# One layer of a hybrid decoder trunk: gates and projections branch by branch, the output projection last, one pool of 4 KB buffers

## The chip, the cores and the metric

The kernel runs on one core of a Trainium2 chip. The metric is the device time in microseconds (us). Three timed executions of the kernel before took 506.86, 507.49 and 507.55 us, so the median is 507.49 us.

## What is computed

The reference is one layer on 512 positions (rows) of 1024 channels, followed by a final RMSNorm:

```
h = RMSNorm(x);  u = h @ w_in          # split into the inputs, gate paths (z) and gate logits below
ya = pool_mixer(a_x)   * silu(a_z)     # trailing-window means of 2/4/8/16, then a 128x128 mix per group
yb = window_attention  * silu(b_z)     # window 128, 8 query heads, 2 key/value heads, sinks
yc = block_attention   * silu(c_z)     # blocks of 256; at 512 positions this is causal attention, 8 heads
ga, gb, gc = split(sigmoid(gate_logits))            # 3 x 1024 columns
merged = ga * (ya @ w_proj_a) + gb * (yb @ w_proj_b) + gc * (yc @ w_proj_c)
out = RMSNorm(x + merged @ w_out)
```

Every matrix product is done in three float32r products, with each operand split into a rounded high part and the rest: high x high, high x low, low x high (`mm3`).

## The kernel before

Activations lie transposed, channels on the 128 partitions and 512 positions in the free dimension. A weight block is 128x1024 float32 (512 KB). It comes in over SP's DMA queue into one of four raw buffers (`wr`). ScalarE (ACT) casts it into its high part `wh` and VectorE (DVE) subtracts to get the low part `wl` (three buffers each). `weights(name)` keeps this two blocks ahead of the use, and each split block starts the load four blocks further on. The host lays the blocks out in the order in which they are used.

The program has four stages.

1. An opening, whose order is written out by hand (`manual_schedule`, until the seventh input block): loads of x, the first input blocks, RMSNorm.
2. 34 input blocks (`UNITS`). A block is 8 chunks of three matmuls, and the work of both attentions and of the pooling mixer is spread over the chunks by a table (`todo`, `tick`). Keys and queries are copied into place by DMAs on SP's queue (`moves`, L263-266) before the first score can use them.
3. Gates and projections (L525-603), channel block by channel block: for j = 0..7 the three gates (24 matmuls of 512 columns each, sigmoid), then the three projections of 12 matmuls each, and their weighted sum, which is split into `merged[j]`. For j = 1 to 5 the first gate is followed by `project_out(j - 1)`: eight products of three matmuls, each into a PSUM bank of its own turn and added by DVE to `acc`, which holds x.
4. A tail (L606-684): for the last three blocks the output projection is summed in PSUM, and row block by row block DVE adds it to `acc`, ACT squares, GpSimd (POOL) multiplies by the final gain, DVE and ACT scale, and SP stores.

After the opening a planner orders each engine's instructions at build time. It takes the program's order as the priority, and it issues an instruction early when its inputs and its buffer are there. Buffers come from pools with a number of slots per tag. A tile takes any free slot and gives it back after its last reader. Before, 2 KB tiles have the tag `t2` (31 slots), 4 KB pairs the tag `two` (9 slots), the normalised activations `hT` have 16 fixed places, and x, the values `vt` and `acc` follow one another in one place of 20 KB (tag `v`). PSUM has four tags of two banks: `big`, `PV`, `S`, `T`.

Of the kernel before, what the change touches and what calls it, by code (L numbers as in the profile page):

```python
# [14 lines left out]
P = 128  # L15
D = 1024
# [29 lines left out]


def weight_blocks():

    blocks = [(u, 1024) for u in UNITS]  # L50
    late = []
    for j in range(KT):
        blocks.append((("ga", j), 1024))
        if late:
            blocks.append((("wo", late.pop()), 1024))
        blocks += [(("gb", j), 1024), (("gc", j), 1024), (("pab", j), 1024), (("pc", j), 512)]
        if j < KT - TAIL:
            late.append(j)
    blocks += [(("wo", j), 1024) for j in range(KT - TAIL, KT)]
    return blocks  # L60
# [3 lines left out]
def trunk(ctx: ExitStack, tc: tile.TileContext, a, out: bass.AP):  # L64
# [17 lines left out]
    blocks = weight_blocks()  # L82
    index = {name: n for n, (name, _) in enumerate(blocks)}
# [6 lines left out]

    def load_upto(n):
        while done["load"] <= min(n, len(blocks) - 1):
            m = done["load"]
            cols = blocks[m][1]
            nc.sync.dma_start(raw_tile(m)[:, :cols], a["w"][m][:, :cols])
            done["load"] += 1
# [9 lines left out]
    def split_upto(n):  # L106
        while done["split"] <= min(n, len(blocks) - 1):
            m = done["split"]
            parts_of(m)
            split_cols(m, slice(0, blocks[m][1]))  # L110
            done["split"] += 1
            load_upto(m + 4)
# [6 lines left out]
    def split(src, name, two=None):  # L119
        hi, lo = (t2(F32R, name + "h"), t2(F32R, name + "l")) if two is None else (two[:, 0, :], two[:, 1, :])  # L120
        nc.scalar.copy(hi, src)
        nc.vector.tensor_sub(lo, src, hi.bitcast(F32))
        return hi, lo

    def mm3(ps, lh, ll, rh, rl, start, stop):
        nc.tensor.matmul(ps, lh, rh, start=start, stop=False)  # L126
        nc.tensor.matmul(ps, lh, rl, start=False, stop=False)  # L127
        nc.tensor.matmul(ps, ll, rh, start=False, stop=stop)  # L128
# [17 lines left out]
    xT = [t2(F32, f"xT{k}") for k in range(KT)]  # L146
# [10 lines left out]
    xn = pool.tile([P, NT, D], F32, name="xn", tag="v", bufs=1, padded_shape=[P, 5, 1024])  # L157
    for t in range(NT):
        nc.sync.dma_start(xn[:, t, :], a["x"][t * P:(t + 1) * P, :])
# [27 lines left out]
    for k in range(KT):  # L187
        hi, lo = t2(F32R, f"xgh{k}"), t2(F32R, f"xgl{k}")
# [22 lines left out]
    def square(t):  # L211
        junk = pool.tile([P, 1280], F32, name=f"junk{t}", tag="p", bufs=2)
        nc.scalar.activation(junk[:, :D], xn[:, t, :], AF.Square, accum_out=small[:, t:t + 1])
# [17 lines left out]
    def normed(k):  # L231
        tmp = t2(F32, f"ht{k}")
        nc.vector.scalar_tensor_tensor(tmp, xT[k], g_sb[:, k:k + 1], rstd_bc, op0=OP.mult, op1=OP.mult)
        hi, lo = const(f"hh{k}", [P, S], F32R), const(f"hl{k}", [P, S], F32R)
        nc.scalar.copy(hi, tmp)
        hT.append((hi, lo, tmp))
# [9 lines left out]
    vt = []  # L246

    def evacuate(u, ps):
# [5 lines left out]
        if kind in ("cq", "ck", "bq", "bk"):  # L254
            hi, lo = split(ps, f"{kind}{i}")
            top, low = slice(0, HD), slice(HD, P)
            if kind[1] == "q":
                two = parts[u] = pair(F32R, f"{kind}{i}two")
                moves = ((two, top, 0, hi, top), (two, low, 0, lo, top),
                         (two, low, 1, hi, low), (two, top, 1, lo, low))  # L260
            else:
                his, los = parts[u] = pair(F32R, f"{kind}{i}his"), pair(F32R, f"{kind}{i}los")
# [4 lines left out]
        elif kind == "cz":  # L267
            full[u] = t2(F32, f"{kind}{i}")
# [5 lines left out]
        else:  # L274
            full[u] = t2(F32, f"{kind}{i}")
# [4 lines left out]
    def value_tile():  # L280
        if not vt:
            vt.append(pool.tile([P, NT, 10, 2, HD], F32R, name="vt", tag="v", bufs=1))
        return vt[0]

    def keep_v(t, ps):

        p3 = ps.rearrange("p (h d) -> p h d", h=8)
        hi, lo = value_tile()[:, t, :8, 0, :], value_tile()[:, t, :8, 1, :]
# [3 lines left out]
    def turn_v(u):  # L292
# [5 lines left out]
        p4 = ps.rearrange("p (t h d) -> p t h d", t=NT, h=2)  # L298
        for n in range(2):
            hi, lo = value_tile()[:, :, 8 + n, 0, :], value_tile()[:, :, 8 + n, 1, :]  # L300
# [19 lines left out]
    def pool_mix(i):  # L320
# [7 lines left out]
        full["oa", i] = t2(F32, f"oa{i}")  # L328
        nc.scalar.activation(full["oa", i], ps, AF.Copy, scale=psc_sb[:, i:i + 1])
# [10 lines left out]
    def head(s):  # L340
        if s not in heads:
# [6 lines left out]
            h.v = n if h.moba else 8 + h.par  # L348
# [43 lines left out]
    def turn(s, b):  # L392
# [19 lines left out]
        hi, lo = t2(F32R, f"pth{s}_{b}"), t2(F32R, f"ptl{s}_{b}")  # L412
# [11 lines left out]
    def weigh(s, half):  # L424
# [9 lines left out]
        for n in (0, 1) if half == 0 else (2, 3):  # L434
            b, j, x, w, q0 = steps[n]
            v = vt[0][:, j, h.v, :, :]
# [3 lines left out]
        if half == 1:  # L440
            kind = "oc" if h.moba else "ob"
            if h.par == 0:
                full[kind, h.block] = t2(F32, f"{kind}{h.block}")
            rest = t2(F32, f"rest{s}")
            nc.scalar.copy(rest[:HD, :], h.o[HD:, :])
            nc.vector.tensor_add(full[kind, h.block][h.rows, :], h.o[:HD, :], rest[:HD, :])

# [23 lines left out]
    for s in range(16):  # L471
# [6 lines left out]
        for half, d in enumerate(WEIGH):  # L478
            at(c + d, weigh, s, half)
    chunk = 15  # L480
# [34 lines left out]
    acc = pool.tile([P, NT, D], F32, name="acc", tag="v", bufs=1, padded_shape=[P, 5, 1024])  # L515
    for t in range(NT):
        nc.gpsimd.dma_start(acc[:, t, :], a["x"][t * P:(t + 1) * P, :])

    fg_two = pair(F32, "fg")
    fg_sb = [fg_two[:, n, :] for n in range(2)]  # L520
# [4 lines left out]
    y = {}  # L525

    def gated(n, i):
        o, z = full["o" + n, i], full[n + "z", i]
        nc.vector.tensor_mul(o, o, z)
        y[n, i] = split(o, f"y{n}{i}")  # L530

    sig_two = {}

    def gate(n, j, sig, m):
        wh, wl = weights(("g" + n, j))
        ps = bank("big", f"ps_g{n}{j}")
        for k in range(KT):
            c = slice(k * P, (k + 1) * P)
            mm3(ps, wh[:, c], wl[:, c], *hT[k], k == 0, k == KT - 1)
        if m == 0:  # L540
            sig_two[j] = pair(F32, f"sig{j}")
        sig.append(sig_two[j][:, m, :] if m < 2 else t2(F32, f"sig{n}{j}"))
        last_sig = nc.scalar.activation(sig[m], ps, AF.Sigmoid)
        if (n, j) == ("c", KT - 1):
            with tc.issue_after(last_sig.ins):
                nc.scalar.sqrt(one, one)

    merged = {}

    def project(j, sig):  # L550
        m = t2(F32, f"m{j}")
        for b, n in enumerate("abc"):
            if b < 2:
                wh, wl = weights(("pab", j))
                at0 = b * 512
            else:
                wh, wl = weights(("pc", j))
                at0 = 0
            ps = bank("T", f"ps_p{n}{j}")
            for i in range(4):  # L560
                c = slice(at0 + i * P, at0 + (i + 1) * P)
                mm3(ps, wh[:, c], wl[:, c], *y[n, i], i == 0, i == 3)
            sg = sig[b]
            if b == 0:
                nc.vector.tensor_mul(m, ps, sg)
            else:
                t = t2(F32, f"t{n}{j}")
                nc.vector.tensor_mul(t, ps, sg)
                nc.vector.tensor_add(m, m, t)
        merged[j] = split(m, f"mg{j}", pair(F32R, f"mg{j}"))  # L570

    turns = [0]

    def out_bank(name):
        turns[0] += 1
        return bank(("S", "PV")[turns[0] % 2], name)

    def project_out(j):
        wh, wl = weights(("wo", j))
        for t in range(NT):  # L580
            for hf in range(2):
                ps = out_bank(f"ps_y{j}_{t}{hf}")
                tc_, c = slice(t * P, (t + 1) * P), slice(hf * 512, (hf + 1) * 512)
# [3 lines left out]
    for j in range(KT):  # L587
        sig = []
        gate("a", j, sig, 0)
        if j == 0:  # L590
            for i in range(4):
                gated("a", i)
        if 0 < j <= KT - TAIL:
            project_out(j - 1)
        gate("b", j, sig, 1)
        if j == 0:
            for i in range(4):
                gated("b", i)
        gate("c", j, sig, 2)
        if j == 0:  # L600
            for i in range(4):
                gated("c", i)
        project(j, sig)


    last = range(KT - TAIL, KT)  # L606
    wo = [weights(("wo", j)) for j in last]
    accs = {}

    ss = const("ss", [P, 48])  # L610
    prod = {}

    def tail_mm(t, hf, js, lo=0, hi=512):
        tc_, c = slice(t * P, (t + 1) * P), slice(hf * 512 + lo, hf * 512 + hi)
        if (t, hf, lo) not in accs:
            accs[t, hf, lo] = bank({0: "S", 1: "PV", 2: "T", 3: "big"}[t] if lo == 0 else "S", f"ps_z{t}{hf}{lo}")
        for j in js:
            mm3(accs[t, hf, lo][:, :hi - lo], merged[j][0][:, tc_], merged[j][1][:, tc_],
                wo[j - last[0]][0][:, c], wo[j - last[0]][1][:, c], j == last[0], j == last[-1])
# [4 lines left out]
    def tail_sum(t, hf, part, lo=0, hi=512):  # L624

        c = slice(hf * 512 + lo, hf * 512 + hi)
        add = nc.vector.tensor_add(acc[:, t, c], acc[:, t, c], accs[t, hf, lo][:, :hi - lo])  # L627
        junk = pool.tile([P, 1280], F32, name=f"sq{t}{part}", tag="p", bufs=2)
        nc.scalar.activation(junk[:, lo:hi], acc[:, t, c], AF.Square, accum_out=col(t, part))
# [4 lines left out]
    def tail_mul(t, hf, eng, lo=0, hi=512):  # L634
        if lo == 0:
# [119 lines left out]
```

## Time and profile before

| what | value |
|---|---|
| median of three executions | 507.49 us |
| the profiled execution | 506.78 us, its span 505.0 us |
| TensorE (PE) busy | 494.8 us, 98% of the span |
| DVE busy | 305.1 us, 60% |
| ACT busy | 232.4 us, 46% |
| POOL busy | 33.3 us, 7% |
| granted TensorE clock | full speed (2.4 GHz) in every slice until the end; mean 0.994 |
| moved by DMA | 59.94 MB, mean 119 GB/s |

The profile counts matmuls as busy until their modelled end, so a busy PE need not be at its peak. What an idle or a waiting engine costs is read from who waits for it.

### The profile page before, as it was taken

The page shows a single profiled execution, that of the slowest core. Times are in us where ns is not written, and L with a number is a line of the kernel's source. Part 1 is how long each engine was busy: PE and PEld are TensorE (multiplying, and loading weights), DVE is VectorE, ACT ScalarE, POOL GpSimd, SP SyncE. Part 2 cuts the span into 40 slices and gives each one's busy share as a digit, 9 for nine tenths or more (in the row PEclk, how much of TensorE's full clock was granted, in tenths as well). Part 3 has the DMA queues.
Part 4 walks back from the last instruction along what each step waited for, and adds up shares of the span by engine and source line. Part 5 has one row for each costly group of instructions (what it writes and reads, how often), then busy time and mean ns, then how long its engine had stood idle before and what let it go on. Part 6 is the DMA issues. An engine that isn't in the chain of part 4 may idle for free.

```text
span 505.0 us, 6455 instructions
## 1 busy us (share of the span) xinstructions
PE 494.8 (98%) x2297; PEld 402.7 (80%) x2297; DVE 305.1 (60%) x605; ACT 232.4 (46%) x452; POOL 33.3 (7%) x72
## 2 busy tenths in 40 slices
PE   8999999999999999999999999999999999999993
PEld 5788888888888888888888887888888888888882
DVE  5558877676788975558556626455272563433376
ACT  6655665656565675559464223132222222323344
POOL 2052000000021100000100000000000000000022
PEclk9999999999999999999999999999999999999997
DMA  8999427743622122210552231313232321313004
GB/s 258 398 257 242 147 74 179 197 125 92 174 72 104 43 83 85 83 56 29 199 182 80 85 123 64 125 65 123 85 104 85 102 85 64 125 64 125 0 2 167
DMA packets 22368, 59.94 MB, mean 119 GB/s; under 512 B 3200, under 2 KB 4224, under 8 KB 22336
## 3 DMA queue, kind: packets, MB, share of 16 engines
q1 hardware_dynamic: 21312, 56.63, 35.6%
q0 software_dynamic: 880, 2.89, 1.6%
q8 instruction: 18, 0.29, 0.2%
q14 instruction: 14, 0.11, 0.1%
q10 hardware_dynamic: 144, 0.00, 0.0%
HBM read 47.98 MB, written 2.10 MB: 99 GB/s over the span
## 4 chain that ended last, share of the span: by engine, by line
PE 95%; DVE 2%; ACT 1%; DMA 1%; issue 0%; SPq 0%; ACTq 0%
PE ps_o L438 3%; PE ps_gc L126 3%; PE ps_gb L126 3%; PE ps_gc L127 3%; PE ps_ga L128 3%; PE ps_gb L127 3%; PE ps_gc L128 3%; PE ps_gb L128 3%; PE ps_ga L127 3%; PE ps_ga L126 3%; PE ps_t L410 3%; PE ps_y L126 2%; PE ps_y L128 2%; PE ps_y L127 2%; PE ps_s L369 2%; PE ps_s L368 2%
## 5 line engine op out<-in xcount | busy, mean ns | idle before, releaser
L103 ACT CAST wh<-wr 128x1024 fp32r<-128x1024 f32 (+2 forms) x88 | 83.5, 952 | 166.5 <-PE ps_gc L127 35.7
L104 DVE TENSOR_TENSOR wl<-wr,wh 128x1024 fp32r<-128x1024 f32 (+2 forms) x84 | 91.6, 1095 | 94.1 <-ACT wh L103 93.7
L377 ACT ACTIVATE p<-p,st 128x128 f32<-128x128 f32 (+2 forms) x64 | 33.4, 523 | 34.5 <-DVE st L375 34.4
L585 DVE TENSOR_TENSOR acc<-acc,ps_y 128x512 f32<-128x512 f32 x40 | 24.8, 684 | 15.7 <-PE ps_y L128 15.7
L421 DVE TENSOR_TENSOR ptl<-ps_t,pth 128x512 fp32r<-128x512 f32 (+3 forms) x56 | 26.5, 476 | 7.3 <-ACT pth L420 6.8
L420 ACT CAST pth<-ps_t 128x512 fp32r<-128x512 f32 (+3 forms) x56 | 23.4, 418 | 12.8 <-PE ps_t L410 7.7
L128 PE MATMUL ps_ga<-hh,wl 128*128 128x512 f32 x64 | 25.3, 395 | 0.0
L127 PE MATMUL ps_ga<-hl,wh 128*128 128x512 f32 x64 | 25.3, 395 | 0.0
L128 PE MATMUL ps_gb<-hh,wl 128*128 128x512 f32 x64 | 25.3, 395 | 0.0
L126 PE MATMUL ps_gc<-hh,wh 128*128 128x512 f32 x64 | 25.3, 395 | 0.0
L127 PE MATMUL ps_gc<-hl,wh 128*128 128x512 f32 x64 | 25.3, 395 | 0.0
L128 PE MATMUL ps_gc<-hh,wl 128*128 128x512 f32 x64 | 25.3, 395 | 0.0
L126 PE MATMUL ps_gb<-hh,wh 128*128 128x512 f32 x64 | 25.3, 395 | 0.0
L127 PE MATMUL ps_gb<-hl,wh 128*128 128x512 f32 x64 | 25.3, 395 | 0.0
L126 PE MATMUL ps_ga<-hh,wh 128*128 128x512 f32 x64 | 25.3, 395 | 0.0
L637 POOL TENSOR_TENSOR yo<-acc,fg 128x512 f32<-128x512 f32 x5 | 6.4, 1294 | 241.7 <-DVE acc L627 239.4
L410 PE MATMUL ps_t<-ident,p 128*128 128x128 f32 x136 | 21.3, 272 | 0.0
L390 DVE TENSOR_SCALAR p<-p,st 128x128 f32<-128x128 f32 (+2 forms) x64 | 19.9, 358 | 0.5
L410 PEld LDWEIGHTS ps_t<-ident,p 128*128 128x128 f32 x136 | 16.7, 141 | 3.7
L438 PE MATMUL ps_o<-pth,vt 128*128 128x256 f32 (+1 forms) x64 | 17.8, 296 | 0.0
L438 PE MATMUL ps_o<-ptl,vt 128*128 128x256 f32 (+1 forms) x64 | 17.7, 300 | 0.0
L375 DVE CUSTOM_DVE_ANT_0 p<-ps_s,mask_c,nscale 128x128 f32<-128x128 f32 (+3 forms) x32 | 16.5, 545 | 1.7 <-PE ps_s L369 1.6
(390 smaller groups left out, 1263.4 us busy)
## 6 DMA issues: line engine op xcount, KB each, us to landing
wr<-in_w SPq DMA_DIRECT2D x72, 512.0 KB, 3.3
xT<-in_xT SPq DMA_DIRECT2D x8, 256.0 KB, 4.7
xn<-in_x SPq DMA_DIRECT2D x4, 512.0 KB, 8.7
wr<-in_w SPq DMA_DIRECT2D x8, 256.0 KB, 2.6
acc<-in_x POOLq DMA_DIRECT2D x4, 512.0 KB, 6.5
out<-yo SPq DMA_DIRECT2D x8, 256.0 KB, 2.3
wr<-in_w SPq DMA_DIRECT2D x8, 128.0 KB, 4.4
ck0his<-ck0h SPq DMA_DIRECT2D x4, 128.0 KB, 6.0
```

The costliest lines, as they stand in the source:

```text
L103: nc.scalar.copy(w_hi[n][:, c], raw_w[n][:, c])
L104: (nc.gpsimd if 4 <= n < 8 else nc.vector).tensor_sub(w_lo[n][:, c], raw_w[n][:, c], w_hi[n][:, c].bitcast(F32))
L126: nc.tensor.matmul(ps, lh, rh, start=start, stop=False)
L127: nc.tensor.matmul(ps, lh, rl, start=False, stop=False)
L128: nc.tensor.matmul(ps, ll, rh, start=False, stop=stop)
L377: exps.append(nc.scalar.activation(dst, dst, AF.Exp, bias=h.st[:, i:i + 1], scale=-1.0, accum_out=h.st[:, 4 + i:5 + i]))
L390: nc.vector.tensor_scalar_mul(dst, dst, h.st[:, 12 + i:13 + i])
L410: nc.tensor.transpose(ps[:, x:x + P], h.p[:, off:off + P], ident)
L420: nc.scalar.copy(hi[:, c], ps[:, c])
L421: nc.vector.tensor_sub(lo[:, c], ps[:, c], hi[:, c].bitcast(F32))
L438: nc.tensor.matmul(h.o[:, q0:q0 + w], v, h.pt[b][e][:, x:x + w], start=n == 0 and e == 0, stop=n == 3 and e == 1)
L585: nc.vector.tensor_add(acc[:, t, c], acc[:, t, c], ps)
```

## The change

The weight blocks are the same, in another order of use, and the projections' blocks are read two at a time (`p`, two blocks of 512 columns in one transfer of 512 KB, rows of 2 KB). For each branch a, b, c the program now makes the gated inputs, and then four times two gates (48 matmuls) and two projections (24 matmuls). The weighted sum of the branches is kept in four tiles `ms`. All eight channel blocks of `merged` exist before the output projection begins. This then runs over j with one open PSUM bank for each of the eight pieces of the output. The piece of the last 128 rows and last 512 columns is added to `acc` after j = 4, since the tail handles it in two halves in other banks. The tail itself is unchanged but for the tiles' names.

The tags `two` and `v`, the places of `hT` and most users of `t2` go into one tag `u` of 35 slots of 4 KB; `t2` keeps 4 slots. The loads of `acc` and of the final gain `fg` stand in the program behind the gates. There is a second form of the gates too (`gate_pair7`, `sums_ready`, `sums_late`, the accumulating loads), behind a flag that is `False`, so none of it is built.

```diff
-        return pool.tile([P, S], dt, name=name, tag="t2", bufs=31)
-
-    def pair(dt, name):
-        return pool.tile([P, 2, S], dt, name=name, tag="two", bufs=9)
+        return pool.tile([P, S], dt, name=name, tag="t2", bufs=4)
+    def unit(dt, name, shape=(2, S)):
+        return pool.tile([P, *shape], dt, name=name, tag="u", bufs=35)
+    def halves(dt, name):
+        u = unit(dt, name)
+        return u[:, 0, :], u[:, 1, :]
...
+STRASSEN = False
+def weight_items():
+    items = [(u, 1024) for u in UNITS]
+    for n in "abc":
+        for p in range(4):
...
+                items += [(("g" + n, 2 * p + f), 1024) for f in range(2)]
+            items.append((("p" + n, p), 1024))
+    return items + [(("wo", j), 1024) for j in range(KT)]
...
+    def project(n, p, sig):
+        wh, wl = weights(("p" + n, p))
+        if n == "a":
+            ms[p] = unit(F32, f"m{p}")
+        for f in range(2):
+            j, m = 2 * p + f, ms[p][:, f, :]
+            ps = bank("T", f"ps_p{n}{j}")
+            for i in range(4):
+                c = slice(f * 512 + i * P, f * 512 + (i + 1) * P)
+                mm3(ps, wh[:, c], wl[:, c], *y[n, i], i == 0, i == 3)
+            if n == "a":
+                nc.vector.tensor_mul(m, ps, sig[:, f, :])
+            else:
+                t = t2(F32, f"t{n}{j}")
+                nc.vector.tensor_mul(t, ps, sig[:, f, :])
+                nc.vector.tensor_add(m, m, t)
+            if n == "c":
+                merged[j] = split(m, f"mg{j}")
+    for n in "abc":
+        gated(n)
...
+        for p in range(4):
+            project(n, p, (gate_pair7 if STRASSEN else gate_pair)(n, p))
+    acc = [unit(F32, f"acc{t}", (D,)) for t in range(NT)]
     for t in range(NT):
-        nc.gpsimd.dma_start(acc[:, t, :], a["x"][t * P:(t + 1) * P, :])
+        nc.gpsimd.dma_start(acc[t], a["x"][t * P:(t + 1) * P, :])
+    fg_sb = halves(F32, "fg")
...
-    def project_out(j):
-        wh, wl = weights(("wo", j))
+    for j in range(KT - TAIL):
+        wo[j] = weights(("wo", j))
         for t in range(NT):
             for hf in range(2):
-                ps = out_bank(f"ps_y{j}_{t}{hf}")
...
-                mm3(ps, merged[j][0][:, tc_], merged[j][1][:, tc_], wh[:, c], wl[:, c], True, True)
-                nc.vector.tensor_add(acc[:, t, c], acc[:, t, c], ps)
+                tail_mm(t, hf, [j])
+    c31 = slice(512, 1024)
+    nc.vector.tensor_add(acc[3][:, c31], acc[3][:, c31], accs.pop((3, 1, 0)))
+    for j in last:
+        wo[j] = weights(("wo", j))
```

## Rows read from the trace of the kernel before

**Rows 1.** The page's first part: busy us, share of the span, instructions.

```profile
PE 494.8 (98%) x2297; PEld 402.7 (80%) x2297; DVE 305.1 (60%) x605; ACT 232.4 (46%) x452; POOL 33.3 (7%) x72
```

**Rows 2.** Waits of PE alone: waiter, releaser, us in total, times, longest us.

```profile
PE ps_warm L141 <- DVE zero L138: 1.1, 1, 1.1
PE acc L127 <- DVE xgl L190: 0.3, 1, 0.3
PE acc L126 <- ACT wh L103: 0.3, 1, 0.3
```

**Rows 3.** Windows: length; PE, PEld, DVE, ACT, POOL busy; clock, DMA share, GB/s.

```profile
40.00:50.00 10.00, 10.00 (x47) 8.16 (x46) 8.96 (x13) 6.02 (x8) 0.45 (x3) 1.00 0.96 246
...
160.00:170.00 10.00, 10.00 (x50) 8.29 (x49) 9.77 (x26) 6.01 (x14) 2.24 (x7) 1.00 0.12 43
...
260.00:480.00 220.00, 220.00 (x946) 176.82 (x945) 104.33 (x134) 61.46 (x80) 0.00 (x0) 1.00 0.27 90
```

**Rows 4.** PE's timeline (start us, us): where output-projection stretches begin and end.

```profile
311.95 0.39 PE L126 MATMUL ps_y<-wh,mg 128*128 128x512 f32 x1
...
317.52 0.39 PE L126 MATMUL ps_gb<-hh,wh 128*128 128x512 f32 x1
...
479.72 0.40 PE L126 MATMUL ps_z<-wh,mg 128*128 128x512 f32 x1
...
494.15 0.28 PE L126 MATMUL ps_z<-wh,mg 128*128 128x256 f32 x1
```

**Rows 5.** The page's groups by line: busy us, mean ns of one, idle before, releaser.

```profile
L104 DVE TENSOR_TENSOR wl<-wr,wh 128x1024 fp32r<-128x1024 f32 (+2 forms) x84 | 91.6, 1095 | 94.1 <-ACT wh L103 93.7
L585 DVE TENSOR_TENSOR acc<-acc,ps_y 128x512 f32<-128x512 f32 x40 | 24.8, 684 | 15.7 <-PE ps_y L128 15.7
```

**Rows 6.** Timelines of PE and DVE where the first gate begins.

```profile
250.41 0.40 PE L126 MATMUL ps_ga<-hh,wh 128*128 128x512 f32 x1
...
255.06 0.69 DVE L122 TENSOR_TENSOR ya3l<-oa,ya3h 128x512 fp32r<-128x512 f32 x1
```

**Rows 7.** The page's DMA issues: count, KB each, median us to landing.

```profile
wr<-in_w SPq DMA_DIRECT2D x72, 512.0 KB, 3.3
...
acc<-in_x POOLq DMA_DIRECT2D x4, 512.0 KB, 6.5
```

**Rows 8.** Timelines of ACT and DVE in the third pooling window.

```profile
158.62 0.58 ACT L276 COPY ax<-acc_ax 128x512 f32<-128x512 f32 x1
...
162.03 0.69 DVE L314 SCALAR_TENSOR_TENSOR pooled<-xs,ax 128x512 f32<-128x512 f32 x1
...
163.86 0.58 ACT L445 COPY rest<-ps_o 64x512 f32<-64x512 f32 x1
```

**Rows 9.** POOL's timeline: its loads; in brackets the idle time before, releaser.

```profile
136.20 1.11 POOL L522 DMA_DIRECT2D fg<-in_fg  x2 [24.82 <-PE ps_s L369]
...
150.92 0.57 POOL L323 DMA_DIRECT2D pw_raw<-in_pool_w  x1
...
247.36 2.15 POOL L517 DMA_DIRECT2D acc<-in_x  x4 [19.39 <-PE ps_o L438]
```

**Rows 10.** SP's and PE's timelines and the DMA issues at the first score.

```profile
39.17 3.21 SPq L266 DMA_DIRECT2D ck0los<-ck0l  x4
...
47.39 0.25 PE L368 MATMUL ps_s<-ck0his,cq0two 128*128 128x192 f32 x1
...
ck0los<-ck0l SPq DMA_DIRECT2D x4, 128.0 KB, 6.1
```

**Rows 11.** Timelines of PE, POOL and DVE in the tail.

```profile
496.16 0.28 PE L128 MATMUL ps_z<-wh,mg 128*128 128x256 f32 x1
...
496.36 1.26 POOL L637 TENSOR_TENSOR yo<-acc,fg 128x512 f32<-128x512 f32 x1 [0.36 <-DVE ss L643]
...
496.39 1.25 DVE L644 SCALAR_TENSOR_TENSOR ss<-ss 128x1 f32<-128x1 f32 x1
...
500.26 0.22 DVE L644 SCALAR_TENSOR_TENSOR ss<-ss 128x1 f32<-128x1 f32 x1
```

More of the change, by code (lines that the diff above doesn't have):

```diff
@@ L145, in trunk @@
     nc.scalar.dma_start(g_sb, a["norm_g"])
-    xT = [t2(F32, f"xT{k}") for k in range(KT)]
+    xT = [h for k in range(0, KT, 2) for h in halves(F32, f"xT{k}")]
     for n in range(2):
@@ L156, in trunk @@
     load_upto(3)
-    xn = pool.tile([P, NT, D], F32, name="xn", tag="v", bufs=1, padded_shape=[P, 5, 1024])
+    xn = [unit(F32, f"xn{t}", (D,)) for t in range(NT)]
     for t in range(NT):
-        nc.sync.dma_start(xn[:, t, :], a["x"][t * P:(t + 1) * P, :])
+        nc.sync.dma_start(xn[t], a["x"][t * P:(t + 1) * P, :])
     sink_sb = const("sink_sb", [P, 8])
@@ L245, in trunk, with kept @@
     pw = []
-    vt = []
+    vt = {}
+    def kept(kind, i):
+        if i % 2 == 0:
+            full[kind, i], full[kind, i + 1] = halves(F32, f"{kind}{i}")
+        return full[kind, i]
     def evacuate(u, ps):
@@ L267, in evacuate @@
         elif kind == "cz":
-            full[u] = t2(F32, f"{kind}{i}")
+            kept(kind, i)
             with tc.issue_after(exps[-1].ins):
@@ L274, in evacuate @@
         else:
-            full[u] = t2(F32, f"{kind}{i}")
+            if kind[1] == "z":
+                kept(kind, i)
+            else:
+                full[u] = t2(F32, f"{kind}{i}")
             nc.scalar.copy(full[u], ps)
@@ L435, in weigh @@
             b, j, x, w, q0 = steps[n]
-            v = vt[0][:, j, h.v, :, :]
+            v = h.v(j)
             for e in range(2):
@@ L442, in weigh @@
             if h.par == 0:
-                full[kind, h.block] = t2(F32, f"{kind}{h.block}")
+                kept(kind, h.block)
             rest = t2(F32, f"rest{s}")
@@ L479, in trunk @@
             at(c + d, weigh, s, half)
+    if STRASSEN:
+        for i2, c in enumerate((244,256)):
+            at(c, sums_ready, i2)
     chunk = 15
@@ L512, in trunk, with gated, sigmoid @@
     assert not todo, sorted(todo)
-    acc = pool.tile([P, NT, D], F32, name="acc", tag="v", bufs=1, padded_shape=[P, 5, 1024])
+    y, merged, ms = {}, {}, {}
+    def gated(n):
+        for i in range(4):
+            o, z = full["o" + n, i], full[n + "z", i]
+            nc.vector.tensor_mul(o, o, z)
+            y[n, i] = split(o, f"y{n}{i}")
+    def sigmoid(out_, in_, last=False):
+        ins = nc.scalar.activation(out_, in_, AF.Sigmoid)
+        if last:
+            with tc.issue_after(ins.ins):
+                nc.scalar.sqrt(one, one)
@@ new lines, in gate_pair, with rows_part @@
+    def gate_pair(n, p):
+        sig = unit(F32, f"sig{n}{p}")
+        for f in range(2):
+            wh, wl = weights(("g" + n, 2 * p + f))
+            ps = bank("big", f"ps_g{n}{p}{f}")
+            for k in range(KT):
+                c = slice(k * P, (k + 1) * P)
+                mm3(ps, wh[:, c], wl[:, c], *hT[k], k == 0, k == KT - 1)
+            sigmoid(sig[:, f, :], ps, (n, p, f) == ("c", 3, 1))
+        return sig
+    def rows_part(k0, c):
+        return [(hT[k][0][:, c], hT[k][1][:, c]) for k in range(k0, k0 + 4)]
@@ new lines, in sums_late, with gate_pair7, product, total @@
+    def sums_late():
+        for i in range(4):
+            hi, lo = (t[:, 256:] for t in hT[i])
+            raw = sums[4, i // 2][:, i % 2, :]
+            nc.scalar.copy(hi, raw)
+            nc.vector.tensor_sub(lo, raw, hi.bitcast(F32))
+    def gate_pair7(n, p):
+        sig, sn = unit(F32, f"sig{n}{p}"), unit(F32, f"sn{n}{p}", (4, 256))
+        left, right = slice(0, 256), slice(256, 512)
+        pa, pb, pd = bank("big", f"ps_ga{n}{p}"), bank("PV", f"ps_gb{n}{p}"), bank("S", f"ps_gd{n}{p}")
+        def product(ps, part, half, h, start):
+            wh, wl = weights(("g" + n + part, p))
+            for i in range(4):
+                c = slice(half * 512 + i * P, half * 512 + (i + 1) * P)
+                mm3(ps[:, left], wh[:, c], wl[:, c], *h[i], start and i == 0, i == 3, not start)
+            return ps[:, left]
+        def total(q):
+            return [(sums[q][0][:, i, :], sums[q][1][:, i, :]) for i in range(4)]
+        nc.scalar.copy(sn[:, 0, :], product(pa, "A", 0, rows_part(0, left), True))
+        nc.scalar.copy(sn[:, 3, :], product(pd, "S13", 0, total(3), True))
+        nc.scalar.copy(sn[:, 1, :], product(pa, "S24", 0, total(2), False))
+        c11 = product(pb, "A", 1, rows_part(4, left), True)
+        nc.vector.tensor_add(sig[:, 0, left], c11, sn[:, 0, :])
+        nc.scalar.copy(sn[:, 2, :], product(pa, "S13", 1, total(1), False))
+        nc.vector.tensor_sub(sig[:, 1, right], sn[:, 3, :], sn[:, 2, :])
+        sigmoid(sig[:, 0, left], sig[:, 0, left])
+        c21 = product(pd, "D", 0, rows_part(0, right), False)
+        nc.vector.tensor_sub(sig[:, 1, left], c21, sn[:, 1, :])
+        c12 = product(pa, "S24", 1, rows_part(4, right), False)
+        sigmoid(sig[:, 1, :], sig[:, 1, :])
+        sigmoid(sig[:, 0, right], c12, (n, p) == ("c", 3))
+        return sig
@@ L523, in trunk @@
                                               ap=[[0, P], [1, 512]]))
[L525 to L570, printed above, removed]
@@ L587, in trunk @@
[L587 to L606, printed above, removed]
@@ L607, in trunk @@
-    wo = [weights(("wo", j)) for j in last]
-    accs = {}
-    ss = const("ss", [P, 48])
+    last = list(range(KT - TAIL, KT))
+    accs, wo = {}, {}
     prod = {}
```

159 lines of the change are left out of this document (102 added, 57 removed).

## The prediction

> **What bounds the kernel now.** I read the page's busy times first, then the waits of PE alone, then the windows by stage, then PE's timeline where one kind of matmul follows another. The first view says that PE is busy for 494.8 of 505.0 us [rows 1]. That alone proves little, since ends of matmuls are modelled. The second view is the strong one: over the whole execution PE waits for other engines three times, 1.7 us in all, and all three belong to the first microseconds (the warm-up matmul and the first two input blocks) [rows 2]. So no PSUM bank, no weight block and no vector result was ever late after the start. The windows agree: from 260 to 480 us, the stage that the change rewrites, PE is busy for 220.00 of 220 us while DVE has 104.33 and ACT 61.46 us of work and the DMA engines are used to 0.27 [rows 3]. The kernel is a stream of matmuls at the chip's pace, and behind the last matmul (start 496.16, 0.28 long) stand 8.6 us of tail on DVE, ACT and the store [rows 11]; 505.0 - 494.8 - 8.6 leaves 1.6 us in which PE is idle at the start. Only the count and pace of matmuls, a new wait of PE, or another tail can move the time.
>
> **The change part by part.**
>
> *Matmul count.* Gates: 24 blocks of 24. Projections: 24 of 12. Output projection for j = 0 to 4: 5 of 24; tail: 63 of 512 columns and 18 of 256. Each number is the same in the new text, only the order differs. Cost 0.
>
> *Matmul pace.* In the old `project_out` 24 matmuls took from 311.95 to 317.52, 232.1 ns each; in the tail 63 took from 479.72 to 494.15, 229.0 ns each [rows 4]. The new j = 0 to 4 loop has the tail's form (PSUM sums that stay open, no DVE add behind each), so I give it the tail's pace: 120 x (232.1 - 229.0) = 0.37 us gained. The other end is no gain at all, 0.
>
> *The 40 adds of `project_out`.* They go: 24.8 us of DVE [rows 5]. PE did not wait for them [rows 2], so this is worth 0. One add (684 ns) remains, for the last piece after j = 4. Behind it on DVE's queue stands the low part of the last weight block (mean 1.095 us [rows 5]), which can only start when block 4's buffers are free, since there are three. The block's cast, which I take as equally long, runs beside the add, so with 0.3 us for the hand-over the chain is some 2.5 us, against 24 matmuls of blocks 5 and 6 (24 x 229 ns = 5.5 us) that PE has meanwhile. Hidden with 3.0 us to spare; without cover it would cost 2.5.
>
> *Weight blocks.* One 512 KB block per 24 matmuls throughout, or 94 GB/s, where the stage now moves 90 [rows 3]; landing takes 3.3 us [rows 7], the load is issued some four blocks (22 us) ahead. The two-block transfers have rows of 2 KB instead of 4 KB: even at twice the landing time they are hidden. Splits: 44 full ones instead of 40 full and 8 half, on DVE and ACT with half their time free. Cost 0.
>
> *First projection.* It used to come after three gates, now after two: 48 matmuls from 250.41, so at 261.6 us. Its last input, `ya3l`, ended at 255.75 [rows 6]. Margin 5.9 us; the inputs of b and c, now needed 67 and 134 us later, gain slack. Sigmoid and products free PSUM banks within about 1 us where the bank is needed again 2.8 us later or more. Cost 0.
>
> *Eight open banks.* The first product in a `T` bank follows 12 matmuls (2.8 us) after the last projection, which needs one DVE product to leave; `big` is long free. The tail finds `merged[7]` made a whole output stretch (120 x 229 ns = 27 us) earlier, but the old one was in time too. Cost 0.
>
> *One pool of 35.* Counting live 4 KB units chunk by chunk from the program, I find at most 29, where the seventh block-attention head is turned (8 for `hT`, 4 values, 4 + 3 keys and queries of the two attentions besides the two shared key tiles and their value tile, 2 branch outputs, 1 temporary, 4 turned probabilities). Without the early loads the pool never binds. With `t2` at 4, a pooling window needs its input, two partial sums or one and the result, three at a time, and `rest` of a head as the fourth: in the third window input 158.62, result 162.03, `rest` 163.86 [rows 8]. Four slots just do, in the stretch where DVE is at 9.77 of 10 us [rows 3]. Value 0; bounds 0 to 3 us (a window late by one, three times).
>
> *Loads of `acc` and `fg`.* These are moved in time, not only in the text. The load of `fg` stood behind everything in the program, yet ran at 136.20, when a 4 KB slot came free; `acc` ran at 247.36, when the values' place came free [rows 9]. In the new pool there are free units from about 40 us on, so I expect 2 MB of `acc` and 0.5 MB of `fg` on POOL's queue as soon as the hand-written opening ends. They hold 5 units from then on (29 + 5 = 34 of 35: it fits), and they meet the stretch from 40 to 50 us in which the DMA engines are already at 0.96 [rows 3]. Each landing may be late there. At 246 GB/s these 2.6 MB are 10.6 us of all engines' time. The tightest user is the first score at 47.39, which needs the copies of `ck0los` whose issue began at 39.17 and which take 6.1 us to land [rows 10]; by the program it needs the first two of the four, the second issued at about 39.17 + 3.21 / 4 = 40.0 and landed at 46.1, so some 1.3 us remain. Bounds: 0 (the copies are ahead in the queues) to 4.8 us (landing doubled, 6.1 - 1.3). I take 0, since weight blocks have their 22 us and only this one wait is tight.
>
> That row says that transfers issued on SP are slow when the engines are full. The Trainium skill, page "DMA: Bandwidth & Descriptors", section "Queues, rings and completion order", goes further: every DMA engine takes turns between the queues that have work, packet by packet, so a load on POOL's queue does not wait behind SP's copies. By that rule the upper half of the bounds is the likelier one; no run here shows it yet.
>
> **Sum.** 506.78 us of the profiled execution, less 0.37, makes 506.4. That execution is 0.71 below the median of the three shown, so on the median's footing 507.49 - 0.37 = 507.1 us.
>
> **The rivals.**
>
> A, slower: the early loads collide. Place: the first scores around 47 us and the copies of the second key block right behind. PE stops, in order, until the copies land. It decides as soon as `acc` is issued before about 45 us. Price up to 4.8 us, I take the middle, 2.5: 509.6. For it: `fg` shows that such loads are issued as early as a buffer allows [rows 9]. Against: the copies were issued before POOL gets to it, and PE's queue has the value block's matmuls to go on with only up to the score.
>
> B, slower: the pool or the four `t2` slots run full and ACT's copies out of PSUM queue behind a missing buffer, so that turned probabilities come late and PE waits. 34 of 35 says that it can. Price up to 3 us: 509.
>
> C, faster: the tail comes in another order. Its critical chain holds a one-element DVE instruction of 1.25 us that takes 0.22 elsewhere; it began at 496.39, just as POOL's product of 1.26 us began at 496.36, and ended with it [rows 11]. If the planner happens to place POOL's product otherwise, about 1.0 us goes: 507.1 - 1.0 = 506.1. Against: the tail's program is the same. The Trainium skill, page "SBUF — State Buffer", section "Who interferes with whom", states this as an exclusive lock between GpSimd and a DVE instruction with two SBUF inputs; the rows agree (1.25 beside 1.26 us).
>
> That the change does not do what it says: the flagged second form of the gates is not built, so no arithmetic is saved; it is part of the forecast.
>
> **How the numbers follow.** Forecast 0.55, A 0.18, B 0.08, C 0.19. About 0.2% (1.0 us) is what a measurement of this kernel can tell from no change, so the forecast's band is 506.5 to 508.5. Faster 0.19 (C), same 0.55, slower 0.26 (A and B). For 8 in 10 the range takes C down to 505.6 and A up to 510.2 (its price plus part of B's).
>
> **What would show it.** Right: PE's waits again only in the first microseconds; matmul starts in the new output stretch 229 ns apart; no wait at the first `T` bank and none at the first projection. A: a wait of PE on a `ck0` copy near 47 us with `acc` loads before it. B: waits of ACT for PE or DVE at `rest`, `ax` or the turned tiles, followed by PE's. C: the last matmul at the same distance from the start but a tail below 8 us. I am wrong altogether if the pace of gates and projections changes (220 us for 946 matmuls, 233 ns each [rows 3]): 864 matmuls at the tail's 229 would be 3.5 us less. Nothing in the trace tells me why they should.

## The result and the profile after

The change made the kernel slower: 510.15 us (median of 8 runs, 509.19 to 511.58) against 507.40 us (8 runs), a ratio of 1.0056 with an interval of 1.0043 to 1.0069. The profiled execution took 509.51 us with a span of 507.7, against 506.78 and 505.0 before.

To see where the 2.7 us of span lie, I took the start of the first matmul of each stage from PE's timelines of both kernels:

| | before, us | after, us | difference added in the stage before it |
|---|---|---|---|
| first `acc_ax` (pooled branch's input) | 130.31 | 130.45 | +0.14 |
| first `acc_az` | 163.53 | 165.65 | **+1.98** |
| first `ps_ga` (first gate) | 250.41 | 252.27 | -0.26 |
| last matmul | 496.16 | 498.59 | **+0.57** |
| end | 505.01 | 507.73 | **+0.29** |

So almost three quarters (1.98 of 2.72 us) were lost in a stage that the diff hardly touches, 90 us ahead of the new gate order.

The page's first part and the waits of PE alone (waiter, releaser, us in total, times, longest), as in [rows 1, 2]:

```profile
PE 495.5 (98%) x2297; PEld 402.8 (79%) x2297; DVE 281.1 (55%) x562; ACT 231.2 (46%) x448; POOL 33.7 (7%) x72
```

```profile
PE ps_mix L170 <- ACT pw L164: 1.8, 1, 1.8
PE ps_warm L185 <- DVE zero L182: 1.1, 1, 1.1
PE acc L171 <- DVE xg L234: 0.3, 1, 0.3
```

DVE has 24.0 us less to do and PE is no sooner done, as forecast. But one wait is new: the first product of the pooling mix waits for the cast of its weights `pw`. The chain of waits around it names what came last (start us, us, what):

```profile
152.00 3.85 DMA pw_raw<-in_pool_w
155.85 0.02 issue
155.88 0.62 ACT pw L164
156.50 0.04 issue
156.54 0.50 PE ps_mix L170
```

The timelines show how one and the same product came to wait in one kernel and not in the other. The kernel before, first ACT, then PE (the load was issued at 150.92 [rows 9] and took 3.6 us, so it was there at 154.5):

```profile
154.06 1.05 ACT L103 CAST wh<-wr 128x1024 fp32r<-128x1024 f32 x1 [0.50 <-ACT pth L420]
155.01 0.26 ACT L420 CAST pth<-ps_t 128x128 fp32r<-128x128 f32 x1
...
156.06 0.61 ACT L121 CAST pwh<-pw_raw 128x512 fp32r<-128x512 f32 x1
...
156.62 0.40 PE L128 MATMUL acc_ax<-hh,wl 128*128 128x512 f32 x1
156.86 0.39 PE L126 MATMUL ps_mix<-po0h,pwh 128*128 128x512 f32 x1
```

The changed kernel, POOL, ACT and PE:

```profile
152.00 0.58 POOL L373 DMA_DIRECT2D pw_raw<-in_pool_w  x1 [1.11 <-DVE st L434]
...
153.28 0.36 ACT L469 CAST pt<-ps_t 128x256 fp32r<-128x256 f32 x1
155.88 0.62 ACT L164 CAST pw<-pw_raw 128x512 fp32r<-128x512 f32 x1 [2.23 <-DMA pw_raw<-in_pool_w]
156.40 0.26 ACT L469 CAST pt<-ps_t 128x128 fp32r<-128x128 f32 x1
...
154.32 0.39 PE L171 MATMUL acc_ax<-h,wh 128*128 128x512 f32 x1
156.54 0.50 PE L170 MATMUL ps_mix<-po,pw 128*128 128x512 f32 x1 [1.84 <-ACT pw L164]
```

Three things differ. The load, now through one of four slots, is issued 1.1 us later. On ACT its cast stands ahead of a weight block's cast and of the next turned tile, so ACT stops for 2.2 us instead of doing them. And on PE's queue the product stands behind 5 `acc_ax` matmuls after the last pair of scores, where 15 stood before: 10 x 233 ns = 2.3 us earlier. The product is ready at almost the same moment in both (156.5 and 156.9); PE reaches it 2 us too early. From `acc_ax` at 154.32 to it are 2226 ns where 233 would be the pace: 2.0 us.

The second loss, 0.57 us, is pace. The first and the last 512-column start of the output projection (PE's timeline; the second row is the first of 256 columns), as in [rows 4]:

```profile
453.87 0.40 PE L170 MATMUL ps_z<-wh,mg 128*128 128x512 f32 x1
...
496.57 0.28 PE L170 MATMUL ps_z<-wh,mg 128*128 128x256 f32 x1
```

183 matmuls in 42.70 us are 233.3 ns each, where the tail before had 229.0 [rows 4] and `project_out` 231.7 over its five stretches (232.1 in the one of [rows 4]). Of the 0.57 us that is 120 x 1.6 + 63 x 4.3 ns = 0.46; the rest goes with the 864 matmuls of gates and projections, which took 201.60 us instead of 201.51. The window of [rows 3] has no idle time (220.00 of 220 us) and two matmuls fewer:

```profile
260.00:480.00 220.00, 220.00 (x944) 176.75 (x943) 84.82 (x96) 63.83 (x82) 3.28 (x6) 1.00 0.31 101
```

The third, 0.29 us, is the tail, in which nothing of the pairing of [rows 11] has changed (PE, DVE, POOL):

```profile
498.59 0.28 PE L172 MATMUL ps_z<-wh,mg 128*128 128x256 f32 x1
498.64 1.31 DVE L751 SCALAR_TENSOR_TENSOR ss<-ss 128x1 f32<-128x1 f32 x1
498.67 1.27 POOL L744 TENSOR_TENSOR yo<-acc,fg 128x512 f32<-128x512 f32 x1 [0.41 <-issue]
```

The two instructions end together again, 1.31 beside 1.27 us. The Trainium skill, page "SBUF — State Buffer", section "Who interferes with whom", states that a DVE instruction with two SBUF inputs contends with a GpSimd instruction that reads SBUF; the rows agree once more.

Of the 0.29 us only 0.06 lies ahead of ACT's last scaling, which starts 4.61 us behind the last matmul's start in the kernel before and 4.67 in the changed one; 0.23 lies behind it, in the scaling and the store. ACT in the kernel before, then in the changed one:

```profile
500.77 0.72 ACT L650 ACTIVATE yo<-yo,ss 128x512 f32<-128x512 f32 x1 [0.74 <-DVE ss L645]
...
503.26 0.72 ACT L757 ACTIVATE yo<-yo,ss 128x512 f32<-128x512 f32 x1 [0.74 <-DVE ss L752]
```

### The profile page after: what moved, and what is told of

It reads as the page before. It is cut to its first block, busy times and chain, and to the rows that moved or that the text cites. A ratio compares the mean times of both kernels' runs of the same rounds, so it can differ in the third digit from the quotient of the medians.

```text
span 507.7 us, 6410 instructions
## 1 busy us (share of the span) xinstructions
PE 495.5 (98%) x2297; PEld 402.8 (79%) x2297; DVE 281.1 (55%) x562; ACT 231.2 (46%) x448; POOL 33.7 (7%) x72
## 4 chain that ended last, share of the span: by engine, by line
PE 93%; DVE 3%; DMA 2%; issue 1%; ACT 1%; SPq 0%; ACTq 0%; DVEq 0%
PE ps_o L487 3%; PE ps_ga L170 3%; PE ps_gc L171 3%; PE ps_gb L170 3%; PE ps_gc L170 3%; PE ps_gb L172 3%; PE ps_gb L171 3%; PE ps_ga L172 3%; PE ps_gc L172 3%; PE ps_ga L171 3%; PE ps_t L459 3%; PE ps_z L170 2%; PE ps_z L171 2%; PE ps_z L172 2%; PE ps_s L418 2%; PE ps_s L417 2%
## 5 line engine op out<-in xcount | busy, mean ns | idle before, releaser
L141 DVE TENSOR_TENSOR wl<-wr,wh 128x1024 fp32r<-128x1024 f32 (+1 forms) x80 | 91.2, 1143 | 130.3 <-ACT wh L140 129.7
L140 ACT CAST wh<-wr 128x1024 fp32r<-128x1024 f32 (+1 forms) x84 | 82.8, 988 | 165.5 <-PE ps_gb L171 32.3
L470 DVE TENSOR_TENSOR pt<-ps_t,pt 128x512 fp32r<-128x512 f32 (+3 forms) x56 | 26.5, 475 | 7.3 <-ACT pt L469 6.8
L171 PE MATMUL ps_z<-wl,mg 128*128 128x512 f32 (+1 forms) x67 | 25.8, 385 | 0.0
L172 PE MATMUL ps_z<-wh,mg 128*128 128x512 f32 (+1 forms) x67 | 25.8, 385 | 0.0
L170 PE MATMUL ps_z<-wh,mg 128*128 128x512 f32 (+1 forms) x67 | 25.8, 385 | 0.0
L170 PE MATMUL ps_ga<-h,wh 128*128 128x512 f32 x64 | 25.3, 395 | 0.0
L171 PE MATMUL ps_ga<-h,wh 128*128 128x512 f32 x64 | 25.3, 395 | 0.0
L172 PE MATMUL ps_ga<-h,wl 128*128 128x512 f32 x64 | 25.3, 395 | 0.0
L170 PE MATMUL ps_gb<-h,wh 128*128 128x512 f32 x64 | 25.3, 395 | 0.0
L171 PE MATMUL ps_gb<-h,wh 128*128 128x512 f32 x64 | 25.3, 395 | 0.0
L172 PE MATMUL ps_gb<-h,wl 128*128 128x512 f32 x64 | 25.3, 395 | 0.0
L170 PE MATMUL ps_gc<-h,wh 128*128 128x512 f32 x64 | 25.3, 395 | 0.0
L171 PE MATMUL ps_gc<-h,wh 128*128 128x512 f32 x64 | 25.3, 395 | 0.0
```

Source lines behind the costliest of these rows:

```text
L140: nc.scalar.copy(w_hi[n][:, c], raw_w[n][:, c])
L141: (nc.gpsimd if 4 <= n < 8 else nc.vector).tensor_sub(w_lo[n][:, c], raw_w[n][:, c], w_hi[n][:, c].bitcast(F32))
L170: nc.tensor.matmul(ps, lh, rh, start=start, stop=False, skip_group_check=more)
L171: nc.tensor.matmul(ps, lh, rl, start=False, stop=False, skip_group_check=more)
L172: nc.tensor.matmul(ps, ll, rh, start=False, stop=stop, skip_group_check=more)
L470: nc.vector.tensor_sub(lo[:, c], ps[:, c], hi[:, c].bitcast(F32))
```

## The experiments

Theory A: the mix weights, late in the new pool, hold PE for 2 us, and that is most of the loss. Its rivals were the new order of gates, and the place of the load. For each run the gap is the time between the starts of the first `ps_mix` and the matmul before it, less 0.23.

**1. A place of its own for the weights.**

```
-            pw_raw = t2(F32, "pw_raw")
+            pw_raw = const("pw_raw", [P, S])
```

> The changed kernel with one edit: the raw weights of the pooling mix get a buffer of their own, so that their load can be issued at the start. Theory A (late mix weights: in the changed kernel PE stands 2.0 us at the first mix product, because its weights are loaded at 152.0 us and the planner put the product 10 matmuls earlier on PE's queue): the wait is gone, 510.15 - 2.0 = about 508.1 us, PE's waits again only in the first microseconds. Theory B (the new order of gates and projections costs the time, the wait is made up later): no change, 510 us.

509.18 us (508.59 to 510.91), ratio 1.0044 [1.0029, 1.0059]. The gap fell from 2.0 to 0.6 us, as A has it, but of these 1.4 us only 0.97 reached the total (508.1 was expected). The load now ran in the first microseconds (2.63 us), and in the profiled execution PE waited there 1.0 us for `xg`, so that `acc_cq` started at 19.21 instead of 17.71. That the load caused this wait isn't shown: in experiment 2, with the load in its late place, `acc_cq` started late as well, at 18.87.

**2. Six temporary slots.**

```
-        return pool.tile([P, S], dt, name=name, tag="t2", bufs=4)
+        return pool.tile([P, S], dt, name=name, tag="t2", bufs=6)
-        return pool.tile([P, *shape], dt, name=name, tag="u", bufs=35)
+        return pool.tile([P, *shape], dt, name=name, tag="u", bufs=34)
```

> The changed kernel with 6 instead of 4 of the 2 KB slots and 34 instead of 35 units. On POOL's queue the load of the mix weights stands where it stood. Theory A with the missing slot as cause: the load no longer waits for a slot, is issued at about 150.9 instead of 152.0, and PE's wait shrinks from 2.0 to about 0.9 us: 509.0 us. If the place on the queues alone decides: unchanged wait, 510.1 us. Theory B, or a shortage of units: no gain or a loss, 510.1 us or more.

508.78 us (508.28 to 510.64), ratio 1.0034 [1.0020, 1.0047]. POOL issues the load without a wait, PE's wait fell to 0.8 us, the gap to 0.95:

```profile
153.11 0.58 POOL L373 DMA_DIRECT2D pw_raw<-in_pool_w  x1
```

```profile
PE ps_mix L170 <- ACT pw L164: 0.8, 1, 0.8
PE ps_s L418 <- DMA ck0los<-ck: 0.7, 1, 0.7
```

So the wait for a slot is about half of the loss, 1.0 of the 2.0 us. The other half stays: the product still stands behind only 5 `acc_ax` matmuls. The second row of the waits is a surprise: in this execution, the slowest of the six, the first score waited for its copies, just where rival A of the prediction was placed, without any `acc` load near it. The small margin that the prediction read there [rows 10] was used up; what used it up was not looked into.

**3. The old kernel with short-lived tiles in four slots.**

```
+    def ts(dt, name):
+        return pool.tile([P, S], dt, name=name, tag="ts", bufs=4)
-            pw_raw = t2(F32, "pw_raw")
+            pw_raw = ts(F32, "pw_raw")
...
```

> The kernel before with one part of the change alone: the short-lived 2 KB tiles (window inputs, partial sums and results, mix weights, rest, products) get a tag of 4 slots, the others keep 27. Theory A: the first mix product moves 10 matmuls ahead on PE's queue as in the changed kernel, the load waits, and PE stands about 2 us: 509.4 us. Theory B (order of gates): 507.4 us, as before.

516.69 us, ratio 1.0186 [1.0173, 1.0199]. The wait appears in the old kernel, with its old order of gates. The load waits 1.1 us for a slot, and the product stands behind 5 `acc_ax` matmuls, both as in the changed kernel:

```profile
160.15 0.57 POOL L326 DMA_DIRECT2D pw_raw<-in_pool_w  x1 [1.11 <-DVE st L388]
```

```profile
PE ps_bc L231 <- DVE rstd L225: 5.4, 1, 5.4
PE ps_mix L129 <- ACT pwh L124: 1.5, 1, 1.5
```

But the total says nothing: the first of these two waits, 5.4 us, lies in the opening, where the short-lived tiles have 4 slots and the others 27; which of the two was too few wasn't separated. Only the second wait is used.

**4. The old order of gates in the new pool.** The new gate and output functions replaced by those of before, with the order of the weight blocks:

```
-    for n in "abc":
-        gated(n)
...
+    for j in range(KT):
+        sig = []
+        gate("a", j, sig, 0)
...
+        project(j, sig)
```

> The changed kernel with the order of gates, projections and output projection undone, in the new pool. Theory A: the 2.0 us wait stays; the 0.57 us that the stretch from the first gate to the last matmul is longer goes only if the order causes it, not if the buffers' places do: 509.6 or 510.1 us. Theory B: 507.4 us, and no wait.

509.35 us (508.80 to 512.23), ratio 1.0046 [1.0029, 1.0064]: the wait stays (1.9 us), and `ps_y` runs at 233.1 ns and `ps_z` at 233.3. Neither loss comes of the new order.

**5. The product four chunks later, load and cast where the change has them.**

```
...
+            if u[1] == 0:
+                at(chunk_of[u] + MIX, pool_weights)
-            at(chunk_of[u] + MIX, pool_mix, u[1])
+            at(chunk_of[u] + MIX + (4 if u[1] == 0 else 0), pool_mix, u[1])
```

> The changed kernel with one move: the first product of the pooling mix (`ps_mix0`) comes four chunks (12 matmuls) later on TensorE's queue; load and cast of its weights stay where the change has them. Theory A (the 2.0 us stall of TensorE at 154 us is the load of `pw_raw`, late by the four slots of `t2`, met too early by the product): the stall of 2.0 us is gone (at most 0.3 left), `ps_ga` starts at about 250.3 instead of 252.3, and the time is 508.1 us (507.7 to 508.6). Rival (the product waits for something else, or the time sits in the slower pace alone): the stall moves with the product or goes and the time stays at 509.7 to 510.5.

509.59 us (509.07 to 509.70), ratio 1.0046 [1.0034, 1.0058]. A miss, since 508.1 was expected: the gap before the first product went, and other gaps came. PE's waits and ACT's row:

```profile
PE ps_mix L170 <- DVE oc L496: 0.5, 1, 0.5
...
PE ps_mix L172 <- DVE pw L165: 0.4, 1, 0.4
```

```profile
155.92 0.62 ACT L164 CAST pw<-pw_raw 128x512 fp32r<-128x512 f32 x1 [2.67 <-DMA pw_raw<-in_pool_w]
```

ACT still stops, now for 2.7 us, with the turned tile, two exponentials and a weight cast behind it. PE pays for that in three long gaps up to 173 us, about 1.5 us together, and in short ones. From the first `acc_ax` to the first gate it needs 121.7 us, against 119.7 in experiment 6, so the 2.0 us are all still there. The early product was where the loss showed; the load that ACT stops for is the loss.

**6. Load and cast traced 50 and 30 chunks ahead, the product left in place.** The same four slots.

```
...
+            if u[1] == 0:
+                at(chunk_of[u] + MIX - 50, pool_load)
+                at(chunk_of[u] + MIX - 30, pool_split)
             at(chunk_of[u] + MIX, pool_mix, u[1])
```

> The changed kernel with the load of the mix weights and their cast traced 50 and 30 chunks ahead of the first product, out of the same four `t2` slots; the product stays where the change has it. Theory A: TensorE waits 0.3 us at most before `ps_mix0`, and the time is 508.1 us (507.7 to 508.6), as with the product moved. Rival B1 (the product waits for the pooled branch on VectorE as well, so that an earlier cast uncovers the next wait): a gap of 0.5 to 1.5 us stays, 508.7 to 509.6. Rival B2 (the early load collides with the score tiles' transfers or holds a `t2` slot that something else then waits for): the wait turns up elsewhere, 509.5 us or more.

507.41 us (506.96 to 507.96, 11 runs), ratio to the kernel before 1.0004 [0.9996, 1.0013]. POOL's, ACT's and PE's rows:

```profile
83.84 0.57 POOL L372 DMA_DIRECT2D pw_raw<-in_pool_w  x1
...
125.69 0.62 ACT L164 CAST pw<-pw_raw 128x512 fp32r<-128x512 f32 x1
...
153.35 0.39 PE L170 MATMUL ps_mix<-po,pw 128*128 128x512 f32 x1
```

The product runs even earlier and nothing waits. This one move takes back the whole difference of the medians, 2.7 us, where 2.0 were expected. In the profiles it takes back 2.13 us, between the first `acc_ax` and the first `acc_az` (35.20 to 33.07 us). A stall can cost more than its length: in the profile of experiment 4 it was followed by slow matmuls (windows of 2 us: length, busy PE, PEld, DVE, ACT, POOL, granted clock, DMA share, GB/s):

```profile
154.00:156.00 2.00, 0.87 (x4) 0.38 (x2) 1.28 (x6) 0.00 (x0) 0.00 (x0) 1.00 0.47 133
156.00:158.00 2.00, 1.27 (x4) 1.04 (x5) 0.89 (x2) 1.94 (x7) 0.00 (x0) 0.78 0.00 0
158.00:160.00 2.00, 2.00 (x7) 1.71 (x6) 1.67 (x3) 1.75 (x3) 1.58 (x3) 0.50 0.00 0
160.00:162.00 2.00, 2.00 (x11) 1.68 (x11) 1.90 (x3) 0.08 (x1) 1.06 (x3) 0.87 0.08 20
```

After a gap of 2.0 us the granted clock fell to 0.50, the 1.2 GHz level, `ps_o` and `acc_ax` started 427 ns apart, and the stage took 36.77 us. The profile of the changed kernel has the same gap, a clock of 1.00 behind it and 35.20 us, so some executions pay these 1.6 us and some don't. Of the seven timed runs of experiment 4 the two with the lowest mean clock (0.993 and 0.991) took 510.81 and 512.23 us, the others at most 509.44. In the changed kernel, though, five of the eight runs have the profiled one's mean clock of 0.996, and their median is 510.23. So the low clock isn't shown to be the reason why the medians differ by more than the profiles; that stays open.

**7. The pace: two unused strips in SBUF.** By the addresses that the build gives them, the weights begin 32 bytes past a multiple of 128 in both kernels. `mg`, which the output projection also reads, begins at 96 in the kernel before and at 64 in the changed one. The strips put it back to 96:

```
+    pad1 = const("pad1", [P, 8])
+    nc.vector.memset(pad1, 0.0)
...
+    pad2 = const("pad2", [P, 24])
+    nc.vector.memset(pad2, 0.0)
```

> The changed kernel with two unused strips in SBUF (32 bytes ahead of the unit pool, 96 bytes ahead of `wh`), so that the units (`mg`, `h`, `y`) begin 96 bytes past a multiple of 128 and `wh` 32, as `merged` and `wh` did in the kernel before; no instruction of the work changes. Theory P (the pace of the output projection follows the place of its operands in SBUF): its matmuls start 229 ns apart instead of 233.3, over some 192 matmuls 0.8 us, so 509.4 us (508.9 to 509.8), while the stall of 2.0 us before `ps_mix` stays. Rival (the pace comes of the tail's order or of eight open banks): 233.3 ns stays, and 510.15 us (509.7 to 510.5).

> The early load and cast and the two strips together. If stall and pace are separate terms they add: 510.15 - 2.0 - 0.8 = 507.35 us (506.9 to 507.9), level with the kernel before within 0.2%. If the pace doesn't follow the place, 508.1; if the early load only moves the wait, 509.4.

With the stall left in: 510.85 us (509.45 to 511.33), ratio 1.0070 [1.0056, 1.0083], where 509.4 was expected. In its profile the stall was longer (2.5 us of waiting) and the low clock followed. With the early load as well: **506.49 us** (506.09 to 507.94, 11 runs), ratio 0.9991 [0.9983, 1.0000], the fastest version of all, and below the 506.9 to 507.9 expected. In both the pace is 229.0 ns; the second's rows:

```profile
451.37 0.39 PE L170 MATMUL ps_z<-wh,mg 128*128 128x512 f32 x1
...
493.27 0.28 PE L170 MATMUL ps_z<-wh,mg 128*128 128x256 f32 x1
```

41.90 us for 183, 0.80 less than in the changed kernel, which is the size expected; the medians of experiments 6 and 7 differ by 0.92. Gates and projections stayed at 233.3 ns (201.60 us for 864), though the strips move their `h` from 64 to 96 as well.

**8. The reverse: the old kernel with `mg` moved from 96 to 64.** One strip of 96 bytes ahead of its pool:

```
     rstd_bc = const("rstd_bc", [P, S])
+    pad = const("pad", [P, 24])
+    nc.vector.memset(pad, 0.0)
```

> The kernel before with one unused strip of 96 bytes ahead of the pool of `mg`, so that `mg` begins 64 bytes past a multiple of 128 (`wh` stays at 32), as in the changed kernel; no instruction of the work changes. Theory P: the output projection's matmuls start 233.3 ns apart instead of 229 to 231, 192 x 2 to 4 ns, so 0.4 to 0.8 us slower: 507.75 to 508.15. Rival (the pace comes of something else that the strips of the new pool moved): 229.1 ns for `ps_z` stays, and 507.35.

```profile
479.89 0.40 PE L126 MATMUL ps_z<-wh,mg 128*128 128x512 f32 x1
...
494.59 0.28 PE L126 MATMUL ps_z<-wh,mg 128*128 128x256 f32 x1
```

63 in 14.70 us, 233.3 ns, and `project_out` takes 233.3 ns too (24 in 5.60 us from 281.09): the pace follows the place, in both kernels and both ways. But the total did not follow: 507.06 us (11 runs), ratio 0.9994 [0.9986, 1.0003], where 0.4 to 0.8 us more were expected. The first gate to the last matmul did take 0.56 us longer (246.31 against 245.75); against that, `acc_ax` to the first gate took 0.35 less (119.75 against 120.10), and the tail 0.17 less. The strip moves other tiles too. What the place is worth over a whole kernel therefore stays open.

**9. The order alone, with stall and pace out of the way.** The fastest version of 7 with the edit of 4.

> The new pool with the early mix weights and the two strips (the version at 506.49 us), but gates, projections and output projection in the old order. With stall and pace out of the way this isolates the order. Theory O (the order is worth nothing, as the run of the old order in the new pool suggests): 506.5 us (506.1 to 506.9). Rival (the longer tail of the new order, 9.1 against 8.85 us from the last matmul's start, is a cost of the order): 506.2 us, with `ps_y` and `ps_z` at 229 ns.

507.12 us (506.36 to 508.35), ratio 0.9996 [0.9987, 1.0005], against 0.9991 [0.9983, 1.0000] for the new order: slower than either expectation, but within the measurement. The profiles tell more. From the first gate to the last matmul the new order needs 245.42 us and the old one 245.78, 0.36 more, because `project_out` keeps its slower pace at place 96, 232.1 ns, where all 183 matmuls of the new loop take 229.0. The first of its stretches, and the gate behind it:

```profile
281.01 0.39 PE L142 MATMUL ps_y<-wh,mg 128*128 128x512 f32 x1
...
286.58 0.39 PE L142 MATMUL ps_gb<-h,wh 128*128 128x512 f32 x1
```

Its tail, from the last matmul's start, is 9.03 us beside 9.22; tails vary about as much between versions whose tail is the same, so no cost of the order is shown there.

**10. The old kernel with the early load.** The edit of 6, in the kernel before:

```
...
+                at(chunk_of[u] + MIX - 50, pool_load)
+                at(chunk_of[u] + MIX - 30, pool_split)
```

> The kernel before with the load and the cast of the mix weights 50 and 30 chunks ahead of the product. Theory A (the late load costs only where TensorE meets it too early, and the kernel before has no such wait): no change, 507.35 us (507.0 to 507.7). Rival (the late load costs in the kernel before as well, on ScalarE's queue or in what follows): 505.4 to 506.8.

507.50 us (506.62 to 507.95), ratio 0.9996 [0.9987, 1.0005]. The late load cost the old kernel nothing: its cast stood behind other work on ACT.

## Why the prediction was wrong

I forecast 507.1 us as likeliest, within 0.2% of the kernel before; it is 0.56% slower, and I gave all slower cases together a chance of 0.26. That 510.15 us lies just inside my range (up to 510.2) is luck: that end came of rival A, which is false.

The step that failed is the one headed *One pool of 35*, in its sentence "Four slots just do, in the stretch where DVE is at 9.77 of 10 us. Value 0; bounds 0 to 3 us". The stall measured 2.0 us in the profile, and without it the medians are 2.7 us lower; both are inside the bounds. I counted the slots that the pooling window and `rest` need, and left out a fifth user of the same four, the raw mix weights, though its load stood in [rows 9]. I also priced a missing slot as a late window. What it did was to put a load's landing time of 3.8 us into ACT's in-order queue, with PE one step behind. About half of it was the wait for a slot and the other half the product's earlier place (experiment 2). Rival B came nearest, with 509 us and a chance of 0.08: slots run full, ACT stops, PE waits. But ACT stopped for a late load and not for a missing buffer, and PE waited at the mix product and not at turned probabilities.

*Matmul pace* failed in sign. The 0.37 us to be gained assumed that the new loop runs at the tail's 229 ns. With `mg` at place 96 it does, and experiment 9 shows the gain, 0.36 us. But in the changed kernel `mg` lies at 64, where both forms of loop take 233.3 ns (experiments 7 and 8). There 0.57 us was lost from the first gate to the last matmul, 0.94 away from the forecast. The new pool moved every tile, and I had not listed that as an effect.

The steps that held: matmul count (2297 in both); the 40 adds, DVE 24.0 us lighter and PE no sooner done; weight blocks, first projection and eight open banks, none of which shows among PE's waits; and, but for 0.1 ns, the pace of gates and projections.

Rival A is false. POOL's loads of `acc` and `fg` came late, not early, and no score waited for them in the changed kernel (POOL, then PE):

```profile
379.25 0.55 POOL L696 DMA_DIRECT2D acc<-in_x  x1 [185.39 <-DVE yc L165]
...
386.69 1.10 POOL L699 DMA_DIRECT2D fg<-in_fg  x2 [0.42 <-PE ps_pb L171]
...
47.78 0.25 PE L417 MATMUL ps_s<-ck0his,cq0two 128*128 128x192 f32 x1
```

So the step *Loads of `acc` and `fg`* was wrong too, without a price: their units were not free from 40 us on, as I had counted. The first load waited 185 us, until DVE had split `yc`; in experiment 4, where the loads stand ahead of the gates in the program, they ran from 206 us on, behind waits for `ps_o`. Which tiles held the units wasn't traced. The rule of the Trainium skill that I weighed there (page "DMA: Bandwidth & Descriptors", section "Queues, rings and completion order") was thus not put to a test. Rival C is false too: POOL's product and the one-element instruction met in the tail as before.

What stays open: why cast and product come forward in their queues. Four slots alone bring it about in the old kernel (experiment 3), but with six slots in the new pool the product stays forward (experiment 2), and with an early load it comes forward even in the old kernel with its 31 slots (153.09 us in experiment 10, 156.86 before). Open is also the 0.29 us of the tail, which varies nearly as much between versions with the same tail (8.96 to 9.22 us in experiments 1, 6 and 7).

## What to carry to other kernels

When a pool is cut, list every tile that uses it, loads first: a load that gets its slot late lands later still, and an in-order engine that casts it stops for all behind it. Trace such a load and its cast tens of steps ahead of the use; moving the user back instead only spreads the wait (experiments 5 and 6). Before calling a change of pace a property of a loop, compare where its operands begin; here the place and the form both counted (experiments 8 and 9).

## What was not expected of the hardware

The same matmul (512 columns, same operands and form) started every 229.0 ns or every 233.3 ns, depending on whether its operand `mg` began 96 or 64 bytes past a multiple of 128, with the weights at 32. The gates, whose `h` moved in the same way, stayed at 233.3 ns. Only these two places were tried, so no rule follows.

A single stall of about 2 us could be followed by several matmuls 427 ns apart at a granted clock of 0.50, 1.6 us more in experiment 4, and in other executions by none. The Trainium skill, page "TensorE: Matmul & The Clock Gate", section "Wait — 56ns, not 53.3ns?", gives 426.7 ns for 512 columns at the lower clock, which agrees, and 215.7 at the full one, where no stretch read here came below 229.0.
